# Gates and memory queries of a two-layer mixer in pairs of chunks, by seven half-size products

## The chip, the cores and the metric

The kernel runs on one core of one Trainium2 chip. The metric is device microseconds of one execution. TensorE (PE) multiplies; VectorE (DVE), ScalarE (ACT) and GpSimd (POOL) work on tiles in SBUF and on results in PSUM; SyncE (SP) issues most transfers. Each engine works through its own queue in order, and a transfer is issued either from SP's queue or from POOL's.

## The reference

Two blocks of two layers each run over 512 positions of width 1024. The change touches the second block alone, and in it three of the products with `w_in`: the four memory queries `mq`, their four gates `mg`, and the branch gates `mgate`, three sets of 1024 columns.

```python
def memory_attention(q, mk, mv):
    s = jnp.einsum('bshd,bmhd->bhsm', q, mk) * (MEM_HEAD_DIM ** -0.5)
    return jnp.einsum('bhsm,bmhd->bshd', jax.nn.softmax(s, axis=-1), mv)

def mixer_layer(x, mem, ...):
    h = rmsnorm(x, g_norm)
    z = jnp.einsum('bsd,dn->bsn', h, w_in)
    dq, dk, dv, dg, lq, lk, lv, lg, mq, mg, mgate = jnp.split(z, splits, axis=-1)
    ...
    y_a = (o_a * silu(dg)) @ w_br_diff       # diff attention, 8 heads
    y_b = (o_b * silu(lg)) @ w_br_dil        # dilated attention, 4 heads, 3 groups
    kv = (rmsnorm(mem, g_mem) @ w_mem_kv)
    o_m = memory_attention(mq, kv[0], kv[1]) # 4 heads over 256 memory rows
    y_m = (o_m * silu(mg)) @ w_br_mem
    gates = sigmoid(mgate)                   # 3 branches x 1024
    merged = gates[0] * y_a + gates[1] * y_b + gates[2] * y_m
    return x + merged @ w_out
```

## The kernel before

Everything is kept transposed: a tile holds 128 columns of width by 512 positions, and the input of a layer is eight such tiles. Each matrix operand is held as a high and a low part, `split` (L167 to L175) makes them: ACT casts the high part (L171) and DVE subtracts it from the source (L172). One chunk of 128 output columns is `dense` (L195): 8 input tiles times 3 products (high by high, high by low, low by high), 24 matmuls of 128x512 that all add into one PSUM bank (the matmul itself is at L165).

`weights` (L177) loads a chunk of 128x1024 raw weights by SP (L183) into one of 3 `wr` buffers. In the attention stages it makes the parts with ACT (L186, L188) and a transfer on POOL's queue that adds the raw weights to their negated high part (L187). From the memory stage on (`adding` is off) ACT casts the high part (L190) and the low part is subtracted by DVE twice out of three times and by POOL once (L192). There are 3 `wh` and 4 `wl` buffers. `proj` (L1208) is one chunk with its weights; the result leaves PSUM by a DVE multiplication with `r`, the norm's factor for each position (L1213).

`layer2` (L1180) writes out the order: 8 heads of diff attention, 4 of dilated attention, the keys and values of the memory (`mem_kv`), 4 memory heads (a chunk for `q`, a chunk for the gate, then the attention), and the merge in two parts. Part 0 takes 8 chunks of the first branch's gate, each followed by a 24-matmul product of `y_a` with `wb2` (tile names `a_`). Part 1 takes for each of 8 output chunks two gate chunks, then two products of 12 matmuls. `acc` gathers the sum, DVE multiplying (L1316) and POOL adding (L1318). Then comes `w_out`. Between the chunks `step` puts in pieces of attention work that was posted earlier. The 1,000 us ahead are the first block.

The tile framework orders each engine's queue and puts in the waits. PSUM has four banks for projections, as two `z` tiles of two banks each, that `bank` hands out a half at a time, and four single banks `a`. Other tiles are slots of one pool in SBUF, handed out and given back (`slot`, `release`); a tile waits until the last reader of its slot has finished. The 16 tiles `xs` of the layer's input are held until the gates are done.

## Time and profile before

| what | value |
|---|---|
| time, median of 3 runs (lowest to highest) | 2822.42 us (2820.11 to 2822.55) |
| profiled execution: its time, its span | 2822.53 us, 2820.8 us |
| PE busy | 2753.5 us (98%) |
| DVE, ACT, POOL busy | 58%, 59%, 25% |
| granted TensorE clock, mean | 0.993 |
| first block | 0 to 1018 us |
| second block, layer 0: attention; memory keys; memory heads; part 0; part 1; `w_out` | 1018 to 1548; 1574; 1664; 1745; 1862; 1912 us |
| second block, layer 1, the same stages | 1912 to 2443; 2465; 2553; 2638; 2755; 2805 us |

The span is that of the core's instructions; the execution's own time is 1.7 us longer. The stages are cut by eye where the order of PE's work changes, and each cut is a few microseconds wide, since the pieces that `step` puts in overlap it.

### The profile page before, as it was taken

The numbers are of one execution on the slowest core, as the hardware profiler recorded it, in microseconds if no ns is written. First come the engines' busy times: TensorE is split into PE (matmuls) and PEld (weight loads), VectorE is DVE, ScalarE is ACT, GpSimd is POOL, SyncE is SP. The second block draws the span as 40 slices with busy tenths as digits, with TensorE's granted clock in tenths as the row PEclk, the third lists the DMA queues.
The fourth block names the chain that finished last, engine by engine and source line by source line (L and its number), as shares of the span: only waits on it lengthen the run. The fifth ranks groups of instructions, "written<-read, shape, count | busy, mean of one in ns | idle before, by whom it ended". The sixth has DMA issues, their size and how long they took to land.

```text
span 2820.8 us, 44127 instructions
## 1 busy us (share of the span) xinstructions
PE 2753.5 (98%) x16728; PEld 2435.9 (86%) x16728; DVE 1637.8 (58%) x4078; ACT 1653.4 (59%) x2923; POOL 697.6 (25%) x793
## 2 busy tenths in 40 slices
PE   7999999999999999999999999999999999999997
PEld 7999999999999878888888888888888888888886
DVE  5788774478778446665445662344676452773333
ACT  6676775677777566777555542236777664553233
POOL 5133232323322322221111211222221121211222
PEclk9999999999999999999999999999999999999999
DMA  6655657856566886756766322347765677422331
GB/s 195 138 131 125 141 130 179 194 133 134 131 137 144 207 203 163 163 130 145 170 147 161 106 82 93 108 143 171 157 151 132 153 164 157 142 75 83 105 113 67
DMA packets 136371, 395.32 MB, mean 140 GB/s; under 512 B 13758, under 2 KB 38022, under 8 KB 136030
## 3 DMA queue, kind: packets, MB, share of 16 engines
q0 software_dynamic: 39456, 143.67, 30.5%
q1 hardware_dynamic: 96702, 248.82, 26.2%
q8 instruction: 132, 2.16, 0.3%
q14 instruction: 81, 0.66, 0.1%
HBM read 383.84 MB, written 8.60 MB: 139 GB/s over the span
## 4 chain that ended last, share of the span: by engine, by line
PE 88%; ACT 6%; DVE 4%; issue 1%; DMA 1%; POOL 0%; DVEq 0%; ACTq 0%; SPq 0%
PE z L165 64%; PE a L165 20%; PE a L949 1%; PE a L492 1%; ACT s L992 1%; ACT wl L186 1%; ACT wh L188 1%; ACT L229 1%; DVE s L963 0%; ACT s L171 0%; ACT L1020 0%; DVE s L175 0%; DVE s L172 0%; ACT s L229 0%; ACT s L174 0%
## 5 line engine op out<-in xcount | busy, mean ns | idle before, releaser
L165 PE MATMUL z<-s,wh 128*128 128x512 f32 (+2 forms) x6784 | 1267.7, 334 | 27.1 <-ACT s L174 8.7
L165 PEld LDWEIGHTS z<-s,wh 128*128 128x128 f32 x6784 | 1045.1, 189 | 161.0 <-ACT s L174 8.9
L165 PE MATMUL z<-s,wl 128*128 128x264 f32 (+2 forms) x3392 | 657.8, 333 | 0.0
L165 PEld LDWEIGHTS z<-s,wl 128*128 128x128 f32 x3392 | 525.3, 188 | 62.7
L187 POOL DMA_DIRECT2D wl<-w x242 | 209.7, 867 | 1089.1 <-ACT wl L186 949.5
L188 ACT CAST wh<-wr 128x1024 fp32r<-128x1024 f32 x274 | 286.9, 1047 | 313.4 <-PE z L165 308.4
L165 PE MATMUL a<-s,s 128*128 128x512 f32 (+5 forms) x1900 | 420.3, 336 | 4.2 <-ACT s L171 1.7
L186 ACT ACTIVATE wl<-wr 128x1024 fp32r<-128x1024 f32 x274 | 288.6, 1057 | 92.4 <-PE z L165 88.9
L165 PEld LDWEIGHTS a<-s,s 128*128 128x128 f32 (+1 forms) x1900 | 295.4, 186 | 35.3 <-ACT s L171 5.1
L190 ACT CAST wh<-wr 128x1024 fp32r<-128x1024 f32 x130 | 136.3, 1049 | 281.4 <-PE z L165 169.7
L192 DVE TENSOR_TENSOR wl<-wr,wh 128x1024 fp32r<-128x1024 f32 x86 | 108.0, 1255 | 202.7 <-ACT wh L190 197.2
L172 DVE TENSOR_TENSOR s<-s,s 128x512 fp32r<-128x512 f32 (+6 forms) x272 | 189.1, 708 | 47.7 <-ACT s L171 40.4
L165 PE MATMUL z<-wh,s 128*128 128x256 f32 x1408 | 209.1, 286 | 7.8 <-DVE s L175 7.5
L192 POOL TENSOR_TENSOR wl<-wr,wh 128x1024 fp32r<-128x1024 f32 x44 | 106.0, 2410 | 438.4 <-ACT wh L190 336.1
L165 PEld LDWEIGHTS z<-wh,s 128*128 128x128 f32 x1408 | 188.0, 191 | 16.0 <-DVE s L175 11.1
L171 ACT CAST s<-s 128x512 fp32r<-128x512 f32 (+6 forms) x272 | 149.9, 565 | 79.2 <-PE a L165 15.5
L172 DVE TENSOR_TENSOR s<-a,s 128x512 fp32r<-128x512 f32 (+3 forms) x266 | 150.4, 584 | 78.6 <-ACT s L171 77.3
L165 PE MATMUL a<-s,wh 128*128 128x512 f32 x768 | 188.8, 393 | 0.0
L1213 DVE TENSOR_TENSOR s<-z,s 128x512 f32<-128x512 f32 x128 | 87.8, 687 | 169.9 <-PE z L165 153.5
L165 PEld LDWEIGHTS a<-s,wh 128*128 128x128 f32 x768 | 144.0, 188 | 33.4
L171 ACT CAST s<-a 128x512 fp32r<-128x512 f32 (+3 forms) x266 | 126.1, 503 | 65.7 <-PE a L949 37.3
L963 DVE CUSTOM_DVE_ANT_0 s<-a,reg 128x512 f32<-128x512 f32 x160 | 108.0, 686 | 40.7 <-PE a L165 39.3
(256 smaller groups left out, 3178.0 us busy)
## 6 DMA issues: line engine op xcount, KB each, us to landing
wr<-w SPq DMA_DIRECT2D x308, 512.0 KB, 3.9
wl<-w POOLq DMA_DIRECT2D x242, 512.0 KB, 5.8
wr<-wo SPq DMA_DIRECT2D x48, 512.0 KB, 3.5
wl<-wo POOLq DMA_DIRECT2D x32, 512.0 KB, 5.7
wr<-wb SPq DMA_DIRECT2D x32, 512.0 KB, 3.4
reg<-tab SPq DMA_DIRECT2D x24, 448.0 KB, 4.5
s<-x SPq DMA_DIRECT2D x16, 264.0 KB, 6.0
r<-s SPq DMA_DIRECT2D x16, 256.0 KB, 3.6
```

The costliest lines, as they stand in the source:

```text
L165: self.nc.tensor.matmul(out, lhsT, rhs, start=start, stop=stop)
L171: nc.scalar.copy(hi, src)
L172: nc.vector.tensor_tensor(lo, src, hi.bitcast(F32), ALU.subtract)
L186: nc.scalar.mul(lo, raw, -1.0)
L187: nc.gpsimd.dma_start(lo, src, accum_op=ALU.add)
L188: nc.scalar.copy(hi, raw)
L190: nc.scalar.copy(hi, raw)
L192: (nc.gpsimd if self.nw % 3 == 1 else nc.vector).tensor_tensor(lo, raw, hi.bitcast(F32), ALU.subtract)
L229: nc.scalar.activation(r[:, a:b], ps[:, : b - a], AF.Ln, bias=self.eps, scale=1.0 / n)
L492: nc.tensor.transpose(pt[:, h], sm[h // 2][:, h % 2, 128 * c : 128 * c + 128], self.ident)
L963: self.nc.vector.tensor_tensor_reduce(e, ps, bias[:, 3 - i : 7 - i].rearrange("p a b -> p (a b)"), 1.0, LOW, ALU.add, ALU.max, mx)
L1213: nc.vector.tensor_tensor(z[:, :512], ps, r[:, :512], ALU.mult)
```

## The change

The 8 chunks of the memory heads and the 24 of the gates are taken in pairs, 16 in each layer. For a pair the two output chunks and the two halves of the 512 positions form a 2 by 2 block product, with the 1024 rows of width as two halves of 512. `dense2` computes it by seven products in place of eight: each has 12 matmuls of 128x256. That is 84 matmuls of 128x256 for a pair, where there were 48 of 128x512. The weights' sums `s1` to `s4` are made for each pair on POOL (L220), 128x512 each; the seven weight operands are split by ACT and DVE (L171, L172). The products leave PSUM singly, in pieces of 128x256: one copy by ACT, six additions or subtractions by DVE (L241, which is the line of `take`), and the first chunk's first half through ACT at L1423 or L1434.

The sums of the input tiles are the same for all pairs of a layer. `park` makes them once at the layer's start, among the diff attention: 8 loads of `res` by SP (L279), 8 products with the gain and `r` by DVE (L280), 16 sums of 128x256 by POOL (L285 to L288), 16 splits, and 32 writes to DRAM by SP (L273), 8 of 128x256 and 24 of 128x512. `unpark` brings them back by 32 transfers on POOL's queue (L308, L314), among the work of `mem_kv`, into slots that `xs` and others have given up: `xs` is now released before `mem_kv`. Since `r` is in the operands, the multiplication at L1213 falls away for the 32 chunks. The weights of a pair are laid out as quarters on the host, in the order in which the products use them.

```diff
+    def dense2(self, uv, B, bank, first, mid=None):
+        q = lambda t, i: t[:, 512 * i : 512 * i + 512]
+        raw = []
+        for c in uv:
+            raw.append(self.wp.tile([128, 1024], F32, name=self.uid("wr"), tag="wr", bufs=3))
+            nc.sync.dma_start(raw[-1], c)
+        (a21, a22), (a11, a12) = ((q(t, 0), q(t, 1)) for t in raw)
+        ss = [self.slot() for _ in range(4)]
+        s1, s2, s3, s4 = (t[:, :512] for t in ss)
+        for o, a, b in ((s1, a21, a22), (s2, s1, a11), (s3, a21, a11), (s4, s2, a12)):
+            nc.gpsimd.tensor_tensor(o, a, b, ALU.add)
+        W = []
+        for i, src in enumerate((a11, s2, s1, a12, s3, s4, a22)):
+            if i % 2 == 0:
+                w = [self.wp.tile([128, 1024], F32R, name=self.uid(t), tag=t, bufs=n) for t, n in (("wh", 3), ("wl", 4))]
+            W.append([q(t, i % 2) for t in w])
+            self.split(src, *W[-1])
+        self.release(ss)
...
+        def product(out, w, b, start=True):
+            seq = [(k, 0, p) for k in range(4) for p in range(2)] + [(k, 1, 0) for k in range(4)]
+            for i, (k, pw, px) in enumerate(seq):
+                nc.tensor.matmul(
+                    out, w[pw][:, 128 * k : 128 * k + 128], B[b][k][px], start=start and i == 0, stop=i == 11, skip_group_check=not start
+                )
+            return out
...
+        x = product(bank()[:, :256], W[0], "11")
+        take(nc.scalar.copy, h(u, 0), x)
+        p = product(bank()[:, :256], W[1], "2")
+        take(tt, h(u, 1), h(u, 0), p, ALU.subtract)
+        p = product(bank()[:, :256], W[2], "1")
+        take(tt, h(z1, 1), h(u, 1), p, ALU.add)
+        product(x, W[3], "21", False)
+        take(first, h(z1, 0), x)
+        if mid:
+            mid()
+        p = product(bank()[:, :256], W[4], "3")
+        take(tt, h(z2, 1), p, h(z1, 1), ALU.subtract)
+        take(tt, h(z2, 0), p, h(u, 1), ALU.subtract)
+        p = product(bank()[:, :256], W[5], "22")
+        take(tt, h(z1, 1), h(z1, 1), p, ALU.add)
+        p = product(bank()[:, :256], W[6], "4")
+        take(tt, h(z2, 0), h(z2, 0), p, ALU.add)
...
+    def unpark(self, B, park):
+        for m in range(4):
+            ah = self.rslot()
+            for j in range(2):
+                self.nc.gpsimd.dma_start(h(ah, j), park[4 * m, j, :, :256])
...
+            for n, k0, k1 in ((1, "21", "22"), (2, "1", "3"), (3, "2", "4")):
+                p = self.pair()
+                for j in range(2):
+                    self.nc.gpsimd.dma_start(p[j][:, :512], park[4 * m + n, j])
...
-        mk, mv = self.mem_kv(l)
-        self.step(4)
+        self.release(xs)
+        back = self.unpark(B, park)
+        mk, mv = self.mem_kv(l, back)
+        for _ in back:
+            pass
+        self.step(RL)
...
         for h in range(4):
-            q = two_parts(proj())
+            z, g = self.dense2(two(), B, bank, plain, step)
+            q = two_parts(z)
+            self.silu2(g, 512)
             self.step(RL)
-            g = gate(RL)
             db += self.mem_head(h, q, mk, mv, g, yb)
...
-            for m in range(8):
-                gs = []
-                for b in ((0,), (1, 2))[part]:
-                    z = proj()
-                    nc.scalar.activation(z[:, :512], z[:, :512], AF.Tanh, scale=0.5)
-                    gs.append(z)
-                    self.step(RL)
...
+            for m2 in range(4):
+                gs = [gates() for _ in range(part + 1)]
```

The first place is POOL's queue at the end of the memory keys' stage, layer 0 of the second block; `s_` are slots, `park` is the DRAM tile. Before, the rows there are:

```order
L192 TENSOR_TENSOR wl_3320_18997<-wr_3318_18995,wh_3319_18996 128x1024
L192 TENSOR_TENSOR wl_3340_19107<-wr_3338_19105,wh_3339_19106 128x1024
L192 TENSOR_TENSOR wl_3352_19204<-wr_3350_19202,wh_3351_19203 128x1024
L1053 TENSOR_TENSOR s_3356_19239<-s_3356_19239,reg2_13817 128x256 x2
L1053 TENSOR_TENSOR s_3367_19290<-s_3367_19290,reg2_13817 128x256 x2
L192 TENSOR_TENSOR wl_3410_19486<-wr_3408_19484,wh_3409_19485 128x1024
L192 TENSOR_TENSOR wl_3453_19708<-wr_3451_19706,wh_3452_19707 128x1024
L192 TENSOR_TENSOR wl_3509_19933<-wr_3507_19931,wh_3508_19932 128x1024
```

After the change, the last of the 32 transfers and the sums of the first two pairs stand there:

```order
L308 DMA s_3460_19609<-park_2368_13913 128x256 x2
L314 DMA s_3461_19612<-park_2368_13913 128x512
L314 DMA s_3468_19627<-park_2368_13913 128x512
L314 DMA s_3469_19628<-park_2368_13913 128x512
L314 DMA s_3462_19613<-park_2368_13913 128x512
L314 DMA s_3463_19616<-park_2368_13913 128x512
L314 DMA s_3470_19631<-park_2368_13913 128x512
L314 DMA s_3472_19635<-park_2368_13913 128x512
L220 TENSOR_TENSOR s_3499_19782<-wr_3497_19778 128x512
L314 DMA s_3471_19632<-park_2368_13913 128x512
L314 DMA s_3473_19636<-park_2368_13913 128x512
L220 TENSOR_TENSOR s_3477_19644<-s_3476_19643,wr_3475_19641 128x512
```

The sum `s2` of the first pair (the last row shown) has moved to the end of the transfers, all of which are issued ahead of it.

The second place is PE's queue in the first pair of that layer (`z_` are PSUM tiles, the second name after the arrow is the weight operand). Before, a chunk reads like this, with 24 matmuls in a row to one bank:

```order
L165 MATMUL z_3538_20121<-s_2278_13517,wh_3548_20192 128x512
L165 MATMUL z_3538_20121<-s_2279_13518,wh_3548_20192 128x512
L165 MATMUL z_3538_20121<-s_2286_13558,wh_3548_20192 128x512
L165 MATMUL z_3538_20121<-s_2287_13559,wh_3548_20192 128x512
```

After the change the product of `s2` (`wh_3480`, `wl_3481`) ends in bank 1 of the tile, and the product of `a12` (`wh_3482`) begins in bank 0 of the same tile:

```order
L234 MATMUL z_3491_19676<-s_3431_19433,wl_3481_19652 128x256
L234 MATMUL z_3491_19676<-s_3449_19538,wl_3481_19652 128x256
L234 MATMUL z_3491_19676<-s_3465_19620,wl_3481_19652 128x256
L234 MATMUL z_3491_19676<-s_3472_19635,wl_3481_19652 128x256
L234 MATMUL z_3491_19676<-s_3427_19425,wh_3482_19657 128x256
L234 MATMUL z_3491_19676<-s_3428_19426,wh_3482_19657 128x256
L234 MATMUL z_3491_19676<-s_3445_19530,wh_3482_19657 128x256
L234 MATMUL z_3491_19676<-s_3446_19531,wh_3482_19657 128x256
```

The first row of the new product waits for the DVE piece that reads the product before it, and no other matmul stands between the two.

The third place is POOL's queue in part 1. Before, the rows are weight subtractions and the sums into `acc`:

```order
L192 TENSOR_TENSOR wl_3616_20619<-wr_3614_20617,wh_3615_20618 128x1024
L1318 TENSOR_TENSOR s_3510_19961<-s_3510_19961,s_3609_20581 128x512
L192 TENSOR_TENSOR wl_3632_20726<-wr_3630_20724,wh_3631_20725 128x1024
L1318 TENSOR_TENSOR s_3510_19961<-s_3510_19961,s_3613_20614 128x512
L1318 TENSOR_TENSOR s_3526_20061<-s_3526_20061,s_3625_20688 128x512
L192 TENSOR_TENSOR wl_3648_20833<-wr_3646_20831,wh_3647_20832 128x1024
```

After, four sums of 128x512 for each pair are added (L220), and L1318 is L1457:

```order
L220 TENSOR_TENSOR s_3936_22341<-wr_3932_22335,wr_3933_22337 128x512
L220 TENSOR_TENSOR s_3937_22342<-s_3935_22340,wr_3933_22337 128x512
L1457 TENSOR_TENSOR s_3713_20898<-s_3713_20898,s_3893_22022 128x512
L1457 TENSOR_TENSOR s_3713_20898<-s_3713_20898,s_3913_22156 128x512
L220 TENSOR_TENSOR s_3954_22473<-wr_3952_22469 128x512
L1457 TENSOR_TENSOR s_3714_20899<-s_3714_20899,s_3894_22023 128x512
L220 TENSOR_TENSOR s_3955_22474<-s_3954_22473,wr_3953_22471 128x512
L1457 TENSOR_TENSOR s_3714_20899<-s_3714_20899,s_3914_22157 128x512
L220 TENSOR_TENSOR s_3956_22475<-wr_3952_22469,wr_3953_22471 128x512
L220 TENSOR_TENSOR s_3957_22476<-s_3955_22474,wr_3953_22471 128x512
L192 TENSOR_TENSOR wl_3974_22605<-wr_3972_22603,wh_3973_22604 128x1024
L1457 TENSOR_TENSOR s_3741_21096<-s_3741_21096,s_3947_22370 128x512
```

The queue now holds eight additions for the two pairs, the four into `acc`, and about two thirds of a weight subtraction for two output chunks.

## Rows read from the trace of the kernel before

**Rows 1.** The page: span, and busy time of each engine.

```profile
span 2820.8 us, 44127 instructions
...
PE 2753.5 (98%) x16728; PEld 2435.9 (86%) x16728; DVE 1637.8 (58%) x4078; ACT 1653.4 (59%) x2923; POOL 697.6 (25%) x793
```

**Rows 2.** Windows by stage: length, busy times, clock, DMA share, GB/s; both second layers.

```profile
1018.00:1340.00 322.00, 314.38 (x1729) 267.45 (x1728) 196.35 (x452) 228.81 (x372) 70.75 (x82) 0.99 0.67 154
...
1548.00:1574.00 26.00, 25.17 (x205) 24.53 (x204) 19.73 (x37) 12.97 (x22) 8.94 (x6) 1.00 0.40 127
1574.00:1664.00 90.00, 88.87 (x448) 73.92 (x447) 63.21 (x137) 48.45 (x102) 10.12 (x5) 1.00 0.25 82
1664.00:1745.00 81.00, 80.63 (x352) 65.42 (x350) 24.61 (x31) 20.73 (x24) 12.75 (x6) 1.00 0.27 91
1745.00:1862.00 117.00, 117.00 (x506) 94.79 (x505) 40.42 (x51) 34.58 (x42) 34.93 (x21) 1.00 0.34 111
...
1912.00:2230.00 318.00, 309.02 (x1708) 264.62 (x1707) 193.87 (x445) 223.73 (x367) 70.71 (x82) 0.99 0.66 151
...
2465.00:2553.00 88.00, 85.55 (x429) 71.05 (x430) 61.52 (x130) 46.41 (x99) 10.72 (x6) 1.00 0.23 78
2553.00:2638.00 85.00, 84.44 (x370) 68.55 (x369) 26.95 (x37) 22.84 (x30) 11.52 (x6) 1.00 0.26 87
2638.00:2755.00 117.00, 117.00 (x507) 94.86 (x507) 39.41 (x49) 34.94 (x42) 35.24 (x22) 1.00 0.35 113
```

**Rows 3.** Chain that ended last, 1555 to 1760 us: start, length, what.

```profile
1555.04 12.15 PE z L165 x104
...
1727.36 5.55 PE a L165 x24
...
1744.02 11.09 PE z L165 x48
```

**Rows 4.** Lines by shape: busy us, mean ns, then idle before.

```profile
L187 POOL DMA_DIRECT2D wl<-w x242 | 209.7, 867 | 1089.1 <-ACT wl L186 949.5 <-ACT s L1052 39.0 <-DVE s L1213 14.7
...
L192 DVE TENSOR_TENSOR wl<-wr,wh 128x1024 fp32r<-128x1024 f32 x86 | 108.0, 1255 | 202.7 <-ACT wh L190 197.2 <-issue 5.4
L192 POOL TENSOR_TENSOR wl<-wr,wh 128x1024 fp32r<-128x1024 f32 x44 | 106.0, 2410 | 438.4 <-ACT wh L190 336.1 <-issue 50.7 <-PE a L165 39.6
...
L1213 DVE TENSOR_TENSOR s<-z,s 128x512 f32<-128x512 f32 x128 | 87.8, 687 | 169.9 <-PE z L165 153.5 <-ACT s L231 11.4 <-PE a L165 4.8
...
L172 DVE TENSOR_TENSOR s<-s,s 128x512 fp32r<-128x512 f32 x99 | 73.2, 743 | 24.8 <-ACT s L171 21.8 <-PE a L165 3.0
...
L171 ACT CAST s<-s 128x512 fp32r<-128x512 f32 x99 | 59.9, 615 | 35.5 <-PE a L165 15.5 <-DVE s L1144 5.7 <-DVE s L1213 3.8
...
L1318 POOL TENSOR_TENSOR s<-s,s 128x512 f32<-128x512 f32 x32 | 41.3, 1291 | 140.2 <-DVE s L1316 140.2
...
L1054 DVE TENSOR_TENSOR s<-a,s 128x256 f32<-128x256 f32 x32 | 12.9, 414 | 1.3 <-POOL s L1053 1.3
```

**Rows 5.** Timeline, PE, 1572.5 us: start, length, what, idle before and releaser.

```profile
1573.60 1.19 PE L165 MATMUL z<-s,wh 128*128 128x512 f32 x4 [0.83 <-DVE s L175]
```

**Rows 6.** Timeline, all engines, 1637 to 1640.5 us.

```profile
1637.03 2.36 POOL L192 TENSOR_TENSOR wl<-wr,wh 128x1024 fp32r<-128x1024 f32 x1 [16.13 <-ACT wh L190]
...
1637.52 2.43 DVE L282 SCALAR_TENSOR_TENSOR s<-s,s 128x512 f32<-128x512 f32 x1 [1.01 <-ACT s L281]
...
1639.11 1.43 PE L165 MATMUL a<-s,s 128*128 128x512 f32 x8 [0.57 <-ACT s L171]
```

**Rows 7.** Timeline, all engines, 1749 to 1752 us.

```profile
1749.16 2.41 POOL L192 TENSOR_TENSOR wl<-wr,wh 128x1024 fp32r<-128x1024 f32 x1 [5.75 <-issue]
...
1749.84 0.69 DVE L1213 TENSOR_TENSOR s<-z,s 128x512 f32<-128x512 f32 x1 [4.35 <-PE z L165]
```

**Rows 8.** DMA issues: tile pair, queue, count, size, median us to landing.

```profile
r<-s SPq DMA_DIRECT2D x16, 256.0 KB, 3.6
...
s<-r SPq DMA_DIRECT2D x16, 256.0 KB, 3.5
```

More of the change, by code (lines that the diff above doesn't have):

```diff
@@ new lines, in park, with away @@
+    def park(self, l, r, gain, park):
+        nc = self.nc
+        h = lambda t, i: t[:, 256 * i : 256 * i + 256]
+        def away(src, n, i):
+            p = self.pair()
+            self.split(src, p[0][:, :n], p[1][:, :n])
+            for j in range(2):
+                nc.sync.dma_start(park[i, j, :, :n], p[j].bitcast(F32)[:, :n])
+            self.release(p)
+        for m in range(4):
+            t = [self.slot(), self.slot()]
+            for i, k in enumerate((m, m + 4)):
+                nc.sync.dma_start(t[i][:, :512], self.res[k, :, :512])
+                nc.vector.scalar_tensor_tensor(t[i][:, :512], t[i][:, :512], self.col(gain, l, k), r[:, :512], ALU.mult, ALU.mult)
+            yield
+            a, b = t
+            f, g = self.slot(), self.slot()
+            tt = nc.gpsimd.tensor_tensor
+            tt(h(f, 0), h(a, 0), h(a, 1), ALU.subtract)
+            tt(h(f, 1), h(a, 1), h(b, 1), ALU.subtract)
+            tt(h(g, 0), h(b, 1), h(f, 0), ALU.add)
+            tt(h(g, 1), h(b, 0), h(g, 0), ALU.subtract)
+            away(h(a, 0), 256, 4 * m)
+            self.release(a)
+            yield
+            away(b[:, :512], 512, 4 * m + 1)
+            self.release(b)
+            yield
+            away(f[:, :512], 512, 4 * m + 2)
+            self.release(f)
+            yield
+            away(g[:, :512], 512, 4 * m + 3)
+            self.release(g)
+            yield
@@ new lines, in unpark @@
+    def unpark(self, B, park):
+        h = lambda t, i: t[:, 256 * i : 256 * i + 256]
+        for m in range(4):
+            ah = self.rslot()
+            for j in range(2):
+                self.nc.gpsimd.dma_start(h(ah, j), park[4 * m, j, :, :256])
+            B["11"].append((h(ah, 0), h(ah, 1)))
+            B["slots"].append(ah)
+            for n, k0, k1 in ((1, "21", "22"), (2, "1", "3"), (3, "2", "4")):
+                p = self.pair()
+                for j in range(2):
+                    self.nc.gpsimd.dma_start(p[j][:, :512], park[4 * m + n, j])
+                B["slots"] += p
+                for i, k in enumerate((k0, k1)):
+                    B[k].append((h(p[0], i), h(p[1], i)))
+            yield
@@ L1151, in mem_head, with mem_kv @@
         ]
-    def mem_kv(self, l):
+    def mem_kv(self, l, other):
         nc, d = self.nc, self.d
@@ L1171, in mem_kv @@
             mk.append(hl)
+            self.step(RL)
+            if h > 2:
+                next(other)
         mv = []
@@ L1176, in mem_kv @@
             mv.append(v)
+            self.step(RL)
+            next(other)
         self.release(ms)
@@ L1239, in layer2 @@
         ya, yb, da, db = [], [], [], []
+        park = self.dp.tile([16, 2, 128, 512], F32, name=self.uid("park"), tag="park")
+        self.post(self.park(l, r, "g2", park))
         for hp in range(4):
@@ L1293, in layer2, with gates @@
         self.adding = False
-        mk, mv = self.mem_kv(l)
-        self.step(4)
+        B = {k: [] for k in ("11", "21", "22", "1", "2", "3", "4", "slots")}
+        self.release(xs)
[3 more added lines that the diff above has]
+            pass
+        self.step(RL)
+        plain = lambda o, ps: nc.scalar.copy(o, ps)
+        step = lambda: self.step(RL)
+        two = lambda: [chunk(), chunk()]
         for h in range(4):
-            q = two_parts(proj())
+            z, g = self.dense2(two(), B, bank, plain, step)
+            q = two_parts(z)
+            self.silu2(g, 512)
             self.step(RL)
-            g = gate(RL)
             db += self.mem_head(h, q, mk, mv, g, yb)
+        def gates():
+            th = lambda o, src: nc.scalar.activation(o, src, AF.Tanh, scale=0.5)
+            z = self.dense2(two(), B, bank, th, step)
+            th(z[1][:, :512], z[1][:, :512])
+            th(z[0][:, 256:512], z[0][:, 256:512])
+            self.step(RL)
+            return z
         acc, mg = [], []
@@ L1469, in tok_cols, with quarters @@
     return [w[512 * k : 512 * k + 512, c0 : c0 + 256].reshape(4, 128, 256).transpose(1, 0, 2).reshape(128, 1024) for k in range(2)]
+def quarters(w, c0, c1):
+    half = lambda c, k: w[512 * k : 512 * k + 512, c : c + 128].reshape(4, 128, 128).transpose(1, 0, 2).reshape(128, 512)
+    return [np.concatenate([half(c, 0), half(c, 1)], 1) for c in (c1, c0)]
 def weights1(w):
```

52 lines of the change are left out of this document (33 added, 19 removed).

## The prediction

> **What bounds the kernel now.** First the page: PE is busy for 2753.5 of 2820.8 us, every other engine for less than 60% [rows 1]. Then the stages: in part 0 and part 1 PE is busy for the whole window, at full clock, and in the memory heads for 88.9 of 90 us [rows 2]. The reader should see from this that in the stages which the change rewrites only PE's own work counts, and that DVE and POOL are far from full there (40 and 35 us of 117 in part 1), except DVE in the memory heads (63 of 90). Then the chain: in parts 0 and 1 it consists of matmuls alone, 24 of 128x512 in 5.55 us, and where two gate chunks follow each other 48 in 11.09 us [rows 3]. So less PE work shortens the time, as long as nothing takes PE's place.
>
> **What is removed.** A pair is 48 matmuls of 128x512, 11.09 us. The pace of 128x256 is read from the memory keys, 104 of them in 12.15 us, 0.117 us each [rows 3]; half the columns cost half the time, so no fixed cost per matmul eats the smaller size. A pair becomes 84 x 0.117 = 9.8 us and saves 1.26 us. 32 pairs: **-40 us**. This term I hold for certain. Below PE's work, the multiplication by `r` goes (32 x 0.69 us of DVE [rows 4]), off the path.
>
> **What is added, 1: the transfers back.** POOL issues 32 transfers in each layer. The nearest row is the transfer of weights on the same queue, for which POOL is busy 0.867 us [rows 4]; that one adds while it writes and is twice the size. As the second place in the order of instructions shows for PE and the first for POOL, the last 17 issues go to slots that the memory keys' last matmuls free, four sums (1.29 us each by the row of POOL's addition) stand among or behind them, and `s2`, which PE's third product needs, comes after all 17. From the first of these slots to that product PE has about 10.5 us of its own (86 matmuls, counted in its queue, at 0.117 us, with a few longer ones). POOL needs 17 x 0.867 + 4 x 1.29 = 19.9 us, and a cast and a subtraction (0.62 and 0.74 us) follow: 21.3 us, so PE stands for 10.8 us in each layer. If an issue costs 0.61 us in place of 0.867 the stall is 6.4; if it costs nothing there is none, since the sums alone are under the cover. I take 8 per layer, between the first two, as the transfers are plain and half as long: **+16 us**, bounds 0 and +21.6. What is queued behind are the sums of the second pair, on time for PE only if the first stands. That a transfer lands some 3.5 us after its issue [rows 8] lies under the chain of issues.
>
> The Trainium skill, DMA: Bandwidth & Descriptors, section on the anatomy of one DMA by the software path, puts nearly all of a transfer's fixed cost into its completion, and says "You can emit a lot of descriptors before the incremental cost shows up". The trace doesn't agree: POOL is busy for 0.867 us with each of 242 issues [rows 4]. By the rule the sum would be 16 us lower; by the row it stands.
>
> **2: the product that begins where the last one ended.** In 8 of 16 pairs of a layer the product of `a12` follows that of `s2` directly and waits for the DVE piece that reads it (second place in the order). Such a hop has a price in the trace: PE stood for 0.83 us behind one DVE operation and for 0.57 us behind an ACT cast [rows 5, 6]. A piece of 128x256 from PSUM takes DVE 0.41 us [rows 4], so I take 0.65: 16 x 0.65 = **+10 us**, bounds 9 and 13. Nearly all other evacuations have one product (1.4 us) or more of PE work to hide in; the cover fails only where DVE stands in a queue, which is the next term.
>
> **3: DVE and POOL in part 1.** The trace shows that the two exclude each other in one case: a DVE operation on two SBUF tiles of 128x512, whose like takes 0.743 us on the mean [rows 4], took 2.43 us when it began inside a POOL subtraction, and ended behind it [rows 6], while DVE's multiplication of a PSUM tile took its 0.69 us inside another [rows 7]. For two output chunks of part 1 PE needs 2 x 9.8 + 2 x 5.55 = 30.7 us, where it needed 33.3. POOL has 8 new sums and the 4 into `acc`, 12 x 1.29, and two thirds of a weight subtraction of 2.41: 17.1 us. DVE has 14 subtractions for the weights of the pairs and 2 for the merged output, 16 x 0.743, and 1.33 x 1.255 for `wb2`: 13.6 us on two SBUF tiles [rows 4]. Together 30.7 us that can't lie beside each other. Before, it was 4 x 1.29 + 2 x 2.41 + 4 x 1.255 + 2 x 0.743 = 16.5 of 33.3. So the pair of engines goes from half full to full, and the 12 evacuations in DVE's queue stand behind whatever subtraction is blocked. Nothing shows how well the two interleave: from nothing (every evacuation, 12 x 0.41 + 4 x 0.69 = 7.7 us, lies beside a POOL operation) to 5 us (two thirds of these are served while POOL is idle). I take 2 us, near the lower end since PE can run ahead of its queue by a bank: 8 x 2 = **+16 us**, bounds 0 and +40.
>
> **4: the memory heads.** For each pair DVE gets 7 subtractions (5.2 us) and 6 pieces (2.5), and loses two multiplications (1.4) and 1.33 weight subtractions (1.7): +4.6 us, 18.6 for the four. From 63 of 90 us it goes to 82 of about 85 [rows 2], and POOL's 16 sums (20.7 us) block some of it. The attention's own work is in that queue and PE waits for it. I take the saving of these pairs (4 x 1.26 us) as mostly lost, **+4 per layer, +8 us**, bounds 0 and +20. In part 0 DVE has 25 of 81 us, and I take nothing.
>
> **5: parking.** In a layer's attention DVE gets some 18 us (8 products and 16 splits of at most 0.743), POOL at most 16 x 1.29, ACT some 9 us, and SP 40 transfers of up to 256 KB, under 4 us to landing [rows 8]. All is spread over a stretch in which PE is busy for 314 of 322 and 309 of 318 us [rows 2], and no reader is near. A write in SP's queue that waits for its split holds back the raw weights behind it, so it isn't free: **+2 per layer, +4 us**, bounds 0 and +8.
>
> **Sum.** -40 + 16 + 10 + 16 + 8 + 4 = +14 us. The profiled execution took 2822.5 us, its span and 1.7 us around it, and is 0.1 us off the median, so 2837 us. With all lower bounds it is -40 + 9 = -31, 2791 us; with all upper ones -40 + 103 = +63, 2885 us.
>
> **The rivals.** *The waits don't build up* (faster): PE's queue runs far enough ahead that terms 3 and 4 are zero. Then -40 + 10 + 4 and the transfers at 0 to 16: 2797 to 2813 us. For it: DVE's evacuations read PSUM and are not blocked [rows 7], and PE has no idle time in parts 0 and 1 now [rows 2]. Against it: 30.7 of 30.7 us. It decides if the subtractions of a pair are done a whole pair ahead.
>
> *Issues cost POOL next to nothing* and the rest is as in the sum: 2837 - 16 = 2821 us, no change. Against it: the 0.867 us of 242 issues [rows 4]. For it: that row is of transfers that add, and no plain one on this queue is in the trace. It is the case that the Trainium skill's page DMA: Bandwidth & Descriptors would give.
>
> *The exclusion decides* (slower): in part 1 the blocked subtraction holds an evacuation in nearly every product, 4 to 5 us for two output chunks, and the memory heads run at DVE's pace: -40 + 20 + 10 + 36 + 16 + 6 = +48, 2870 us. For it speaks that DVE comes to 82 of 85 us there. Against: POOL and DVE alternate, and each DVE operation is over within 0.75 us.
>
> **How the numbers follow.** A difference of 0.2%, 5.6 us, is about what a measurement of this kernel tells from none: 2816.8 to 2828.1 us is the same. My forecast of 2837 (2828 to 2858) gets 0.37, the waits that don't build up 0.36, the cheap issues 0.15, the exclusion 0.12. So faster 0.36, same 0.15, slower 0.37 + 0.12 = 0.49. Cases of both signs hold most of the chance: the range is 2800 to 2862, which leaves out some 0.08 below and 0.1 above, and the likeliest case's own is 2828 to 2858.
>
> **What would show it.** Pairs of 84 matmuls in 9.8 us wherever PE doesn't wait; a gap of PE of 6 to 11 us at the end of the memory keys, ended by `s2`'s split, with POOL busy at L308 and L314; 16 gaps of some 0.65 us at L234 behind L241; in part 1 windows of 33 us for two output chunks, with DVE subtractions of 1.3 us or more beside L220 and PE waiting behind L241; memory heads no shorter than before. I am wrong if part 1 takes 31 us for two chunks (the exclusion hides), if an issue of the plain transfer is short on POOL, or if the attention stages lengthen by more than 10 us, because SP's queue was held up.

## The result and the profile after

The changed kernel takes 2911.07 us (median of 4 runs, 2909.07 to 2914.41), the kernel before 2822.1 us in the same runs: a ratio of 1.0318, 95% interval 1.0300 to 1.0336. It is 89 us slower. The forecast was slower by 14 us, and the range ended at 2862 us.

The page of the changed kernel:

```profile
span 2909.1 us, 47853 instructions
...
PE 2759.5 (95%) x17880; PEld 2495.3 (86%) x17880; DVE 1870.6 (64%) x4436; ACT 1739.5 (60%) x3179; POOL 907.0 (31%) x995
...
park<-s SPq DMA_DIRECT2D x48, 256.0 KB, 3.2
s<-park POOLq DMA_DIRECT2D x48, 256.0 KB, 4.4
```

The last two rows are the new transfers, 256 KB each, with their time to landing. PE's busy time did not fall [rows 1], although there is less work in the products, and beside it PE stands for 149.6 us (span less busy time) where it stood for 67.3. The windows show where, and with what clock. The columns are as in [rows 2]; the cuts are attention, memory keys, memory heads, part 0, part 1 with `w_out`, of layer 0 of the second block:

```profile
1018.00:1564.00 546.00, 525.97 (x2836) 447.07 (x2835) 313.58 (x702) 346.36 (x581) 119.52 (x138) 0.98 0.72 169
1564.00:1598.00 34.00, 29.65 (x223) 27.88 (x223) 28.81 (x72) 18.61 (x43) 17.70 (x21) 0.93 0.63 200
1598.00:1673.00 75.00, 63.42 (x455) 59.55 (x455) 57.23 (x109) 38.29 (x88) 37.31 (x37) 0.91 0.39 113
1673.00:1768.00 95.00, 92.02 (x568) 82.09 (x568) 59.75 (x97) 40.36 (x75) 26.25 (x17) 0.99 0.29 89
1768.00:1957.00 189.00, 175.10 (x1059) 156.18 (x1058) 118.57 (x163) 78.33 (x130) 88.17 (x55) 0.97 0.41 127
```

In the heads the granted clock is 0.91 and in part 1 with `w_out` 0.97, where it was 1.00 in the windows of the heads and of part 1 before [rows 2]. Three windows in a row around one gap of part 1 show what that is:

```profile
1772.00:1775.00 3.00, 0.49 (x4) 0.29 (x3) 3.00 (x4) 0.81 (x2) 0.98 (x1) 0.86 0.26 63
1775.00:1781.00 6.00, 5.49 (x25) 5.19 (x26) 3.01 (x6) 1.94 (x4) 4.39 (x3) 0.50 0.42 147
1781.00:1790.00 9.00, 9.00 (x77) 9.00 (x77) 6.04 (x12) 4.24 (x9) 0.15 (x1) 1.00 0.24 68
```

PE stands for most of 3 us, then works at 0.50, that is at 1.2 GHz, with 25 matmuls in 6 us, and then at 2.4 GHz with 77 in 9. Over the whole span the mean clock is 0.981:

```profile
core 0: 2909.1 us, clock 0.981
```

(1 - 0.981) x 2909 = 55 us of full speed are missing, against (1 - 0.993) x 2821 = 20 us before. Not all of that is a loss, since in part of the time PE stands anyway. Added up over the stretches at 1.2 GHz, PE is busy for 80.4 of 111 us; before, it was for 19.3 of 36.8. Work at half speed so cost 40 us where it cost 10: some 30 us of the loss are not waits but work at the lower clock behind them. That is also why PE's busy time stayed: 38 us fewer of products, 30 us more by the clock, and each wait leaves the recorded end of a pipelined matmul (0.28 us, at a pace of 0.118) in the busy time. There are 112 waits of more than 0.15 us, where there were 51, so that makes about 10 us.

To compare kernels by stage, the stages are cut in every trace at the same matmuls (the first of the memory keys; the first of the heads' products; the last of part 0; the last of `w_out`). The sums of both layers in us, and the difference from the kernel before:

| kernel | time | attention | keys | heads and part 0 | part 1 and `w_out` |
|---|---|---|---|---|---|
| before | 2822.1 | 1055.5 | 54.6 | 319.5 | 355.8 |
| changed | 2911.1 | +32.0 | +13.8 | +19.7 | +22.7 |
| e1 parking alone | 2851.7 | +29.8 | 0 | 0 | -0.9 |
| e5 e1 without writes | 2840.7 | +16.8 | +0.5 | +0.1 | -0.9 |
| e14 e5, low parts by ACT | 2834.8 | +11.3 | +1.0 | 0 | -0.9 |
| e6 parking later | 2904.2 | +25.2 | +13.3 | +20.7 | +22.6 |
| e2 pairs, no parking | 2849.8 | -1.7 | -2.2 | +14.0 | +19.5 |
| e3 back by SP | 2894.1 | +29.7 | +8.4 | +8.2 | +20.6 |
| e4 no sums of weights | 2867.7 | +29.7 | +14.8 | +6.4 | -5.9 |
| e9 sums on DVE | 2901.9 | +33.0 | +13.6 | +18.6 | +19.5 |
| e15 gates' low parts by ACT | 2878.6 | +32.9 | +12.6 | +14.3 | -3.7 |
| e7 heads' low parts by ACT | 2900.0 | +32.5 | +13.2 | +11.5 | +23.6 |
| e8 first product's bank apart | 2881.8 | +31.1 | +25.8 | -1.0 | +3.2 |
| e13 another product's bank | 2915.8 | +33.7 | +13.5 | +17.5 | +26.9 |
| e10 three mends | 2864.1 | +28.2 | +17.8 | -10.3 | +5.5 |
| e11 products alone | 2807.6 | 0 | -1.9 | +1.1 | -15.5 |
| e12 e11, heads' low by ACT | 2807.2 | -0.3 | -2.3 | +2.0 | -15.5 |

The columns are those of the profiled executions. Those of e3, e7 and e9 took 2889.55, 2903.59 and 2907.95 us, so these rows add up to 4.6 us less, 3.6 and 6.0 us more than the median beside them tells. The two middle columns are best read together, since pieces of attention work move between them: in e8 PE has 550 matmuls in the keys' stages of both layers, in the changed kernel 458.

The products should take 19 us out of each of the last two columns (16 pairs by 1.18 us; a pair is 84 matmuls at 118 ns, 9.91 us). So the changed kernel lost 32 us to the attention, 14 to the keys' stage, and about 39 and 42 us in the two others.

### The profile page after: what moved, and what is told of

Read it like the earlier page. It is cut to its first block, busy times and chain, and to the rows that moved or that the text cites. A ratio compares the mean times of both kernels' runs of the same rounds, so it can differ in the third digit from the quotient of the medians.

```text
span 2909.1 us, 47853 instructions
## 1 busy us (share of the span) xinstructions
PE 2759.5 (95%) x17880; PEld 2495.3 (86%) x17880; DVE 1870.6 (64%) x4436; ACT 1739.5 (60%) x3179; POOL 907.0 (31%) x995
## 3 DMA queue, kind: packets, MB, share of 16 engines
q0 software_dynamic: 48672, 158.36, 31.1%
## 4 chain that ended last, share of the span: by engine, by line
PE 77%; DVE 9%; ACT 6%; issue 3%; DMA 3%; POOL 2%; SPq 0%; DVEq 0%; ACTq 0%; POOLq 0%
PE z L165 49%; PE a L165 17%; PE z L234 7%; DVE s L172 1%; DVE wl L172 1%; PE a L1064 1%; PE a L607 1%; POOL s L1457 1%; POOL s L220 1%; DMA wr<-w 1%; ACT wl L186 1%; DVE s L175 1%; DMA s<-park 1%; DVE s L241 1%; DVE s L1078 1%
## 5 line engine op out<-in xcount | busy, mean ns | idle before, releaser
L165 PE MATMUL z<-s,wh 128*128 128x264 f32 (+2 forms) x5760 | 1017.2, 323 | 26.6 <-ACT s L174 9.4
L165 PEld LDWEIGHTS z<-s,wh 128*128 128x128 f32 x5760 | 852.9, 189 | 114.1 <-ACT s L174 9.7
L165 PE MATMUL z<-s,wl 128*128 128x264 f32 (+2 forms) x2880 | 526.1, 322 | 0.0
L188 ACT CAST wh<-wr 128x1024 fp32r<-128x1024 f32 x274 | 286.9, 1047 | 307.1 <-PE z L165 300.0
L165 PEld LDWEIGHTS z<-s,wl 128*128 128x128 f32 x2880 | 429.7, 188 | 41.2
L234 PE MATMUL z<-s,wh 128*128 128x256 f32 x1792 | 267.2, 293 | 53.6 <-DVE s L241 34.9
L234 PEld LDWEIGHTS z<-s,wh 128*128 128x128 f32 x1792 | 241.9, 197 | 69.1 <-DVE s L241 37.6
L172 DVE TENSOR_TENSOR s<-s,s 128x512 fp32r<-128x512 f32 (+6 forms) x304 | 219.4, 736 | 64.0 <-ACT s L171 47.3
L171 ACT CAST s<-s 128x512 fp32r<-128x512 f32 (+6 forms) x304 | 167.0, 565 | 79.6 <-DVE s L812 10.0
L172 DVE TENSOR_TENSOR s<-a,s 128x512 fp32r<-128x512 f32 (+3 forms) x266 | 149.8, 583 | 71.4 <-ACT s L171 69.9
L171 ACT CAST s<-a 128x512 fp32r<-128x512 f32 (+3 forms) x266 | 126.0, 503 | 63.5 <-PE a L1064 35.4
L234 PE MATMUL z<-s,wl 128*128 128x256 f32 x896 | 148.7, 290 | 5.0 <-DVE wl L172 5.0
L190 ACT CAST wh<-wr 128x1024 fp32r<-128x1024 f32 x66 | 68.9, 1049 | 122.9 <-PE a L165 54.4
L171 ACT CAST wh<-s 128x512 fp32r<-128x512 f32 x128 | 76.3, 618 | 100.3 <-PE z L234 49.6
```

Of the source, the lines that this page charges most:

```text
L165: self.nc.tensor.matmul(out, lhsT, rhs, start=start, stop=stop)
L171: nc.scalar.copy(hi, src)
L172: nc.vector.tensor_tensor(lo, src, hi.bitcast(F32), ALU.subtract)
L188: nc.scalar.copy(hi, raw)
L190: nc.scalar.copy(hi, raw)
L234: nc.tensor.matmul(out, w[pw][:, 128 * k : 128 * k + 128], B[b][k][px], start=start and i == 0, stop=i == 11, skip_group_check=not start)
```

## The experiments

**Parking (e1, e5, e14, e6).** e1 adds only the parking to the kernel before.

```diff
...
+        park = self.dp.tile([16, 2, 128, 512], F32, name=self.uid("park"), tag="park")
+        self.post(self.park(l, r, "g2", park))
```

> The kernel before with the parking alone (sums of the input tiles made and written to DRAM, never read back, chunks as before). If the loss in the attention stages (17.4 and 14.6 us by the stages of the changed kernel) comes from the parking there, its cost is 32 us and the time 2854 us, the stages behind unchanged. The rival is that parking is hidden, as the prediction's 4 us had it, and the attention lost its time to something else that the change does: then 2824 to 2828 us.

Measured: 2851.67 us, ratio 1.0102 (1.0086 to 1.0119). The 29 us are all in the attention. So the parking is not hidden. PE's waits there show which evacuations are late (total us, times, longest). First the kernel before from 1018 to 1546.4 us, where L949 and L996 are the lines that L1064 and L1111 are after the change:

```profile
PE z L165 <- DVE s L175: 3.7, 5, 1.3
PE a L949 <- DVE s L996: 2.7, 3, 1.1
```

Then the changed kernel from 1018 to 1564 us:

```profile
PE z L165 <- DVE s L175: 9.6, 8, 3.6
PE a L1064 <- DVE s L1111: 3.6, 2, 2.3
PE a L1064 <- DVE t L1078: 2.4, 4, 1.4
```

PE waits for DVE's evacuations of the token tiles (L175) and for the attention's softmax, with DVE's added work in the same queue. And SP's queue waits for the splits (e1, the writes are its L214):

```profile
SPq L214 <- ACT s L171: 23.5, 11, 4.9
...
SPq L214 <- DVE s L172: 14.3, 11, 5.3
```

For 38 us of layer 0 SP stands at a write, with raw weights behind it. e5 leaves the writes out of e1:

```diff
-            for j in range(2):
-                nc.sync.dma_start(park[i, j, :, :n], p[j].bitcast(F32)[:, :n])
```

> The kernel before with the parking alone, without its 32 writes a layer (loads, products, sums and splits stay). With the writes it took 2851.7 us, all of the 29 us in the attention stages, where PE waits for DVE. If DVE's added operations there are the cause, the writes don't matter: 2848 to 2853 us. If the writes hold back the raw weights in SP's queue, 2826 to 2835 us.

Measured: 2840.71 us, 1.0066 (1.0051 to 1.0081), between the two expectations: the writes cost 11 of the 29 us. By which path is not shown: in e1 none of PE's waits in layer 0's attention is ended by a weight, the waits for DVE are longer. e14 takes the low parts off DVE as well:

```diff
-            self.split(src, p[0][:, :n], p[1][:, :n])
+            nc.scalar.copy(p[0][:, :n], src)
+            nc.scalar.copy(p[1][:, :n], src)
```

> The kernel before with the parking alone, without its writes, and with the low parts written by ACT as a copy in place of DVE's subtraction (values of no use, nobody reads them). It took 2840.7 us with the subtractions. If DVE's subtractions are what delays PE in the attention, 2824 to 2832 us. If it is the products and loads at the layer's start (the first gaps are there), 2836 to 2842 us.

Measured: 2834.79 us, 1.0047 (1.0032 to 1.0062). The 16 subtractions of each layer are worth 6 us; some 13 us stay for the loads, DVE's 8 products, POOL's sums and ACT's casts, which were not separated. e6 posts the whole parking later in the changed kernel:

```diff
-        self.post(self.park(l, r, "g2", park))
         for hp in range(4):
...
+        self.post(self.park(l, r, "g2", park))
         for hp in range(2):
```

> The changed kernel with the parking posted at the start of the dilated attention in place of the layer's start. DVE was busy for 196 of 322 us in the first part of a layer before the change and for 97 of 208 in the later part. If the parking costs where it falls among DVE's evacuations at the layer's start, it is mostly hidden there: 2885 to 2892 us. If its DVE and SP work costs the same wherever it stands: 2908 to 2914 us.

Measured: 2904.23 us, 1.0291 (1.0275 to 1.0306), between the two expectations. Only 7 us come back. The first waits of the layer are gone, and others stand further on, among them one of 3.8 us behind an evacuation (L1335). A stage whose DVE is busy half the time did not hide it.

**The pairs without the way through memory (e2).** The operands are halves of `xs`:

```diff
...
-        park = self.dp.tile([16, 2, 128, 512], F32, name=self.uid("park"), tag="park")
-        self.post(self.park(l, r, "g2", park))
...
-        self.release(xs)
-        back = self.unpark(B, park)
+        for k in range(4):
+            p = lambda t, i: tuple(x[:, 256 * i : 256 * i + 256] for x in xs[t])
+            for n, (t, i) in {"11": (k, 0), "21": (k, 1), "22": (k + 4, 0), "1": (k + 4, 1), "2": (k, 1), "3": (k + 4, 0), "4": (k + 4, 1)}.items():
+                B[n].append(p(t, i))
...
```

> The changed kernel without parking and without the way back: the products read halves of the input tiles xs, which are held to the end of the gates (the sums of input tiles and the factor r are left out, so the gates and queries have other values; the memory keys' stage has its pieces of attention behind it instead of between). If the preparation of the pairs' weights on POOL, DVE and ACT is what costs in the memory heads and part 1, the attention returns to the time of before (-32 us), the wait for the parked tiles goes (-14 in the keys' stage and some -15 in the first pair of the heads), and the rest stays: 2845 to 2855 us, slower than before. If the pairs cost nothing and parking and unparking are all, the 40 us of the products come out: 2785 to 2795 us.

Measured: 2849.76 us, 1.0095 (1.0080 to 1.0110). The attention and the keys are back at their time, and the two last columns are 14 and 20 us over that of before, where the products should have put them 19 us under it. The loss has two halves that appear without each other: e1 has one of them, e2 the other.

**The way back (e3).**

```diff
-                self.nc.gpsimd.dma_start(h(ah, j), park[4 * m, j, :, :256])
+                self.nc.sync.dma_start(h(ah, j).bitcast(F32), park[4 * m, j, :, :256])
...
-                    self.nc.gpsimd.dma_start(p[j][:, :512], park[4 * m + n, j])
+                    self.nc.sync.dma_start(p[j].bitcast(F32)[:, :512], park[4 * m + n, j])
```

> The changed kernel with the 32 transfers back on SP's queue. If POOL's issues in a row are what the first pair waits for, as the prediction had it (16 us with both layers, and the clock's fall behind it), the time comes to 2885 to 2895 us. If the wait is for the slots and for the landing of the transfers (4 us each), it stays within 2905 to 2920 us, since SP's queue has raw weights behind the same waits.

Measured: 2894.12 us, 1.0252 (1.0236 to 1.0267): 17 us, the time that the first theory gave. The rows of the transfers in the changed kernel (ns least, median, most), PE's waits for them in its whole span, and PE's and POOL's timelines at the first pair of layer 0:

```profile
L314 POOL DMA_DIRECT2D s<-park x48: 527/567/622, 1571.4 to 2544.5; - x48
```

```profile
PE z L234 <- DMA s<-park: 10.8, 6, 3.0
```

```profile
1606.89 0.74 PE L234 MATMUL z<-s,wh 128*128 128x256 f32 x4
1609.94 1.37 PE L234 MATMUL z<-s,wh 128*128 128x256 f32 x4 [2.31 <-DMA s<-park]
1611.11 1.05 PE L234 MATMUL z<-s,wl 128*128 128x256 f32 x4
1614.60 1.21 PE L234 MATMUL z<-s,wh 128*128 128x256 f32 x3 [2.43 <-DMA s<-park]
1616.51 0.58 PE L234 MATMUL z<-s,wh 128*128 128x256 f32 x1 [0.70 <-DMA s<-park]
```

```profile
1612.19 1.10 POOL L314 DMA_DIRECT2D s<-park  x2
1613.30 2.63 POOL L220 TENSOR_TENSOR s<-s,wr 128x512 f32<-128x512 f32 x2
```

An issue holds POOL for 0.57 us, less than the row of the adding transfer; and what PE waited for were the tiles themselves, issued late and 4.4 us on their way (the last two, issued from 1612.19 on, end PE's last wait at 1616.51), not `s2`. But `s2` was close behind them: its sum is the last of the two in the last row and ends at 1615.93, its cast at 1616.59. With the tiles there in time, PE would by these rows still have stood for some 4 of the 5.4 us (an estimate: from 1612.3, where the product of `s2` would have begun without the three waits shown, to that cast).

**The sums of weights (e4, e9, e15).** e4 puts raw quarters in their place:

```diff
-        for o, a, b in ((s1, a21, a22), (s2, s1, a11), (s3, a21, a11), (s4, s2, a12)):
-            nc.gpsimd.tensor_tensor(o, a, b, ALU.add)
+        s1, s2, s3, s4 = a21, a22, a11, a12
```

> The changed kernel without the four sums of each pair on POOL: raw quarters stand in for s1 to s4 (128 additions left out, the pairs' results are others). If POOL's sums, by the exclusion with DVE and by the chain from sum to sum to split, are what costs in the memory heads and part 1, those stages lose most of their 67 us and the time is 2845 to 2860 us. If it is DVE's own load (seven subtractions and six evacuations a pair) or the three buffers of raw weights, it stays at 2890 us or above.

Measured: 2867.68 us, 1.0156 (1.0141 to 1.0171), between the two expectations and nearer to the first: 43 us, 29 of them in part 1. e9 makes them on DVE (`nc.vector` for `nc.gpsimd` in the line above).

> The changed kernel with the four sums of each pair on DVE in place of POOL. Without the sums part 1 was 14 us a layer shorter. If that was the exclusion (subtractions of 0.6 us that took 1.2 to 1.8 beside POOL, sums of 1.3 that took 1.7) and the chain through POOL's queue, part 1 gains some 5 to 8 us a layer although DVE gets 8 more operations for two output chunks, and the heads, where DVE is full, lose 5 to 10: 2900 to 2915 us. If it was the plain work of the sums, DVE is full in part 1 too, and the time is 2930 us or more.

Measured: 2901.93 us, 1.0284 (1.0266 to 1.0302): DVE gets 128 operations more, and the kernel is not slower; the median is 9 us lower (runs of 2897.07 to 2907.95 us against 2909.07 to 2914.41). Part 1 gained 3 us in both layers, less than expected, and the heads lost nothing. e15 leaves POOL's sums and takes the gates' subtractions off DVE (`low` is false for the gates' pairs alone):

```diff
...
-            self.split(src, *W[-1])
+            if low:
+                self.split(src, *W[-1])
+            else:
+                nc.scalar.copy(W[-1][0], src)
+                nc.scalar.copy(W[-1][1], src)
...
```

> The changed kernel with the low weight parts of the gates' pairs written by ACT as a copy in place of DVE's subtraction (their values differ; POOL's sums stay). If DVE standing against POOL is what part 1 loses by, it gains what the run without sums gained there, 14 us a layer: 2880 to 2888 us. If the loss is the chain from raw weights through POOL's sums to the split, 2900 us or more.

Measured: 2878.63 us, 1.0202 (1.0185 to 1.0219): 32 us, 26 of them in part 1, nearly what e4 gained there, with all of POOL's sums in place. So the chain through POOL's sums alone is not the cause (e15 keeps it), and neither is DVE's load alone (e4 keeps it): the loss needs both engines' work, and the rows show the two standing against each other. The rows (busy us, mean ns of one) of the changed kernel:

```profile
L172 DVE TENSOR_TENSOR wl<-s,wh 128x512 fp32r<-128x512 f32 x128 | 117.5, 936 | 26.6 <-ACT wh L171 25.9
L220 POOL TENSOR_TENSOR s<-s,wr 128x512 f32<-128x512 f32 x64 | 99.2, 1551 | 51.7 <-DMA wr<-w 41.6 <-PE a L165 3.8 <-DVE s L172 3.0
```

and of e9, where POOL makes no sums:

```profile
L172 DVE TENSOR_TENSOR wl<-s,wh 128x512 fp32r<-128x512 f32 x128 | 91.7, 730 | 12.2 <-ACT wh L171 11.9
```

A subtraction takes 0.94 us beside the sums and 0.73 without; the prediction had it at 0.743 for all 14 of two output chunks. In part 1 of the changed kernel they alternate, DVE first, POOL below:

```profile
1803.00 1.58 DVE L172 TENSOR_TENSOR wl<-s,wh 128x512 fp32r<-128x512 f32 x1 [0.77 <-ACT wh L171]
1804.51 1.78 DVE L172 TENSOR_TENSOR wl<-wr,wh 128x512 fp32r<-128x512 f32 x1
1806.21 0.41 DVE L241 TENSOR_TENSOR s<-s,z 128x256 f32<-128x256 f32 x1
1806.55 1.44 DVE L172 TENSOR_TENSOR wl<-s,wh 128x512 fp32r<-128x512 f32 x1
```

```profile
1802.75 1.29 POOL L1457 TENSOR_TENSOR s<-s,s 128x512 f32<-128x512 f32 x1
1804.01 1.74 POOL L220 TENSOR_TENSOR s<-wr 128x512 f32<-128x512 f32 x1
1805.70 1.74 POOL L1457 TENSOR_TENSOR s<-s,s 128x512 f32<-128x512 f32 x1
```

The evacuation at 1806.21 takes its 0.41 us beside POOL's sum, but it came out of the queue only after two subtractions of 1.6 and 1.8 us. No row of POOL in either trace reads a PSUM tile (`z` or `a`), so the evacuations are left to DVE and ACT. The Trainium skill, SBUF — State Buffer, section on its two separate sides, says that a DVE instruction with two SBUF inputs contends with a GpSimd one that reads SBUF; these rows agree. How much of the loss is the longer subtractions, and how much is DVE waiting for casts that come late behind POOL's work (26.6 us in the first of the rows, 12.2 in e9), is not separated.

**The heads' subtractions (e7).** The same edit for the heads' pairs alone.

> The changed kernel with the low weight parts of the memory heads' pairs written by ACT as a copy in place of DVE's subtraction (their values are others; the gates' pairs stay). DVE is busy for 67 of 72 us of the heads where nothing is unparked. If DVE's load is the heads' bound, 28 subtractions of 0.6 to 0.9 us leave its queue and the heads shorten by 8 to 14 us a layer: 2883 to 2895 us. If the wait for the parked tiles is what the heads lose, they stay and the time is 2905 us or more.

Measured: 2899.97 us, 1.0277 (1.0261 to 1.0292): 11 us in all, 8 in the heads and part 0 of both layers. DVE's load there costs, but less than the expected 8 to 14 us a layer.

**The shared tile (e8, e13).**

```diff
-        x = product(bank()[:, :256], W[0], "11")
+        x = product(self.a()[:, :256], W[0], "11")
```

> The changed kernel with the first product's bank taken from the four single banks a in place of a half of a z tile, so that the product of a12 no longer waits for the DVE piece that reads the product of s2. The prediction's term was 16 waits of 0.65 us, 10 us: 2898 to 2903 us, with the clock's fall behind them perhaps 2893. If these waits only uncover the next, or PE's order has another product between, 2907 us or more; if the banks a are missed by the attention, slower than 2911.

Measured: 2881.80 us, 1.0212 (1.0195 to 1.0229): 29 us, three times what was expected. PE's waits behind the DVE evacuations, first of the changed kernel from 1560 to 1960 us, then of e8 from 1560 to 1950 us:

```profile
PE z L234 <- DVE s L241: 15.9, 13, 3.9
```

```profile
PE z L234 <- DVE s L241: 5.3, 6, 2.2
```

e13 is the control: `self.a()` for the product of `s1` instead, one bank more, with the tile still shared.

> The changed kernel with the product of s1 in a bank of a, in place of the first product: one bank more as in the run that gained 29 us, but the first product and that of s2 still share a z tile, so that the product of a12 still waits for the evacuation of s2's. If the shared tile is the cause, 2905 us or more. If any further bank gains it, 2880 to 2888 us.

Measured: 2915.78 us, 1.0334 (1.0319 to 1.0350): nothing gained. It is the wait of one product for the evacuation of the product before it. PE's timeline of the changed kernel has it where the prediction put it, at the product of `a12` in 8 pairs of each layer. Nine of these 16 waits are 0.51 to 0.67 us long, five 1.05 to 1.45, and two 3.95 and 4.03; together they are 19.2 us. In e8 the product of `a12` never waits for L241. The rest of the 29 us is the clock behind the waits and other waits for L241, 15.8 us in the changed kernel and 9.5 in e8. The first product's bank is held over four products, and what it gained to take this bank out of the `z` tiles is not separated from the shared tile. One of the two longest cases, with all engines in order of time:

```profile
1843.51 3.42 POOL L1457 TENSOR_TENSOR s<-s,s 128x512 f32<-128x512 f32 x2
...
1844.62 2.85 DVE L172 TENSOR_TENSOR wl<-s,wh 128x512 fp32r<-128x512 f32 x2
...
1846.89 1.73 POOL L220 TENSOR_TENSOR s<-s,wr 128x512 f32<-128x512 f32 x1
1846.96 0.63 ACT L174 ACTIVATE s<-s 128x512 fp32r<-128x512 f32 x1 [3.23 <-POOL s L1457]
...
1847.62 1.55 DVE L175 SCALAR_TENSOR_TENSOR s<-s,s 128x512 fp32r<-128x512 f32 x1
...
1849.10 0.41 DVE L241 TENSOR_TENSOR s<-s,z 128x256 f32<-128x256 f32 x1
...
1849.56 1.22 PE L234 MATMUL z<-s,wh 128*128 128x256 f32 x4 [3.95 <-DVE s L241]
```

PE stood for 3.95 us for an operation of 0.41 us. Ahead of it in DVE's queue were two subtractions, 2.85 us beside POOL's additions into `acc`, and L175. That one needs the cast at L174, which waited 3.23 us for the same additions, and it took 1.55 us beside the sum of POOL. So a chain through POOL takes part in this case: that of `acc`, not that of the sums.

In e8 DVE and POOL still stand against each other (0.87 us for a subtraction of a sum, 1.46 for the most frequent form of POOL's sums), and yet part 1 with `w_out` gained 19.5 us, where e15 gained 26 and e4 29. The two causes are not two losses side by side. From e2 to e11, which has the edits of e4 and e8 together, the time falls by 42 us, and singly they gave 43 and 29. Mending either one wins back about half of the 42 us lost in this stage, or more.

**What is left (e10, e11, e12).** e10 joins e3, e6 and e8.

> The changed kernel with three mends together: the first product's bank from a, the transfers back on SP's queue, the parking among the dilated attention. If the three losses lie apart, they add: 2911 - 29 - 17 - 7 = 2858 us. If they are one loss seen three times (PE waits once for DVE, whoever is late), 2865 to 2880 us. Either way slower than before, since the parking's 22 us and the sums stay.

Measured: 2864.09 us, 1.0151 (1.0135 to 1.0168): 47 us of the 53 that the three gave singly. They lie nearly apart. e11 is e2 with the edits of e4 and e8: products, splits and evacuations alone, and so without the right values.

> The pairs without parking, without the way back, without the sums of weights, and with the first product's bank from a: 84 matmuls a pair as in the change, their low and high weight parts and their evacuations still made (sums of inputs, sums of weights and the factor r left out). If the products' saving of 40 us is real and what remains beside it is small, 2785 to 2795 us. If the seven splits and seven evacuations a pair alone fill DVE in the memory heads, 2800 to 2815 us.

Measured: 2807.60 us, 0.9949 (0.9932 to 0.9965). A stretch without waits in the changed kernel's chain gives the products' pace:

```profile
1746.68 4.25 PE z L234 x36
```

0.118 us each, as forecast (0.117). In e11 they save 15 us of the 38: part 1 and `w_out` gain 15.5 of 19 us, and the heads and part 0 nothing. e12 adds e7's edit to e11.

> The pairs alone (no parking, no way back, no sums), and in the memory heads the low weight parts written by ACT as a copy, so that 28 subtractions a layer leave DVE, which is busy there for 59 of 68 us (the values differ as before, and those low parts too). The products should save 38 us (84 matmuls at 118 ns), the pairs alone saved 15. If DVE in the heads holds back the rest, 2790 to 2798 us. If the rest is lost elsewhere (evacuations in the parts, the clock, short waits), 2803 to 2808 us.

Measured: 2807.24 us, 0.9951 (0.9934 to 0.9968), the same as e11. DVE's subtractions are not what holds the heads there. PE's waits in the heads and part 0 come to 7.3 us in layer 0, none longer than 1.7, where they were 2.3 before; they are spread over ACT's casts, DVE's evacuations and the attention, and which of them could be mended stays open.

## Why the prediction was wrong

The side was right and the size was not: +14 us forecast, +89 measured, which is above the sum of all its upper bounds (2885 us). Two steps failed, the parking and the price of a product's wait for the one before it, and the clock had no term. By its own terms:

- **The products**, -40 us: held in kind. The pace is 118 ns, so -38 us, and the experiments with the products alone show 15 of them.
- **The transfers back**, +16 us: 17 us by e3. That the size fits is luck: an issue is 0.57 us, below both prices that it reckoned with (0.867 and 0.61), and the tiles' landing, said to lie under the chain of issues, is what PE waited for, 10.8 us in both layers, with the clock at 0.52 in the stretch from 1610 to 1620 us.
- **The product that begins where the last one ended**, +10 us, bounds 9 and 13. This step failed in its price. The 16 waits are there, and nine of them cost what it said, but together they are 19.2 us, and to mend them gave 29 (e8 with e13). It took PE's stall behind one DVE operation with nothing ahead of it; in seven of 16 the evacuation stood behind other work in DVE's queue (3.95 and 4.03 us at the longest), and the clock fell behind the longest.
- **DVE and POOL in part 1**, +16 us, bounds 0 and 40: 26 us in that stage by e15. The mechanism is right. But the 30.7 of 30.7 us that can't lie side by side did not set the time by themselves: e8 leaves them in place and gains 19.5 us in that stage, so the term and the one before it count much of the same loss.
- **The memory heads**, +8 us: e7 gives back 8 us in the heads and part 0. That is no confirmation. The term rested on DVE at 82 of 85 us; from the heads' first product to the first product of `y_a` it is busy for 73.9 of 93.2 us in layer 0, and in e12 the same subtractions taken off DVE gave nothing.
- **Parking**, +4 us, bounds 0 and 8: 29 us by e1. This is the largest miss. The step said that no reader is near and spread the work over the stretch; it counted no reader of the queues. The attention's evacuations stand behind the parking's DVE work (PE's waits for L175 went from 3.7 to 9.6 us in layer 0), and its writes cost 11 us (e5), on a path that is not shown. Its own sign of being wrong, attention stages longer by more than 10 us, came true (32 us in both layers), though of the reason that it gave, the held-up SP queue, the writes' 11 us are the most that the runs show.
- **The clock** had no term. Some 30 us of the 89 are work at the lower clock behind PE's gaps, spread over the terms above.

The loss to be explained is 89 + 38 = 127 us, of which e12, with all of these causes taken out, still has 23. For the other 104 single edits gave back 118 us (29 parking, 17, 29, 32 and 11), so they count part of it twice: e4 and e8 overlap by some 30 us in the kernels without parking, e10's three by 6. The list of causes is shown by the edits, their shares are not. Of the rivals, the exclusion that decides (2870 us) named the mechanism of part 1 but not the parking. The cheap issues were wrong in their reason: at 0.57 us an issue is not next to nothing, and cheaper ones alone would have left the landing.

No version with all of the change's work beats the kernel before: the best, e10, takes 2864.09 us. The products alone, with sums, inputs and `r` left out, save 15 us, and the parking alone costs 29.

## What to carry to other kernels

A saving on the bounding engine is worth only what its feeding engines can still supply: count, before the edit, the time in which they exclude each other, and look for the places where the bounding engine waits for one of them with no other work between, since there the two losses meet (one bank changed in e8 won back 29 us with the exclusion nearly as it was). Price a wait on an in-order queue with the work that stands ahead of it, not with the operation waited for, and ask of each parked or posted piece who is queued behind it on every engine that it touches. If PE stands, add what the lower clock costs behind the gaps: here some 30 us beside 82 of standing.

## What was not expected of the hardware

The clock adds a good third to the waits: 82 us more of standing came with some 30 us lost to work at the lower clock. During a gap of 2.5 us the clock fell, and the 6 us behind it ran at 1.2 GHz. And moving 128 additions from the engine with time to spare (POOL, 31% busy) to the one with less (DVE, 64%) did not make the kernel slower (the median is 9 us lower): the most frequent form of sum took 1.55 us on POOL and 0.79 on DVE, and the subtractions fell from 0.94 to 0.73.
